# The MLPs of a decoder trunk: first matrix by weights-stationary columns, woven between the row blocks of the second

## The chip, the cores and the metric

The kernel runs on one core of one Trainium2 chip. The metric is device time in microseconds (us) of one execution; the median of several runs counts. The engines are called as in the profile: PE is TensorE (matmuls), PEld its weight loads, DVE VectorE, ACT ScalarE, POOL GpSimd, SP SyncE, which issues the DMAs of the weights.

## The reference

A decoder trunk of two layers on 256 tokens with a width of 2048, in float32. Layer 0 is a retention layer, layer 1 latent attention (MLA); each is followed by the same kind of MLP, which is what the change is about:

```python
def rms_norm(x, gain):
    y = xf * lax.rsqrt(jnp.mean(xf * xf, axis=-1, keepdims=True) + RMS_EPS)
    return y * gain

def sq_relu_mlp(h, w1, w2):
    return jnp.square(jax.nn.relu(h @ w1)) @ w2      # w1: 2048 x 8192, w2: 8192 x 2048

for layer in range(2):
    x = x + (retention or mla)(rms_norm(x, ...))
    x = x + sq_relu_mlp(rms_norm(x, norm_mlp[layer]), mlp_w1[layer], mlp_w2[layer])
```

## The kernel before

**Precision.** Every float32 operand is split in two fp32r parts, a high part (ACT casts it) and a low part (DVE subtracts): `split`, L180. A product is three matmuls: high by high, high by low, low by high.

**Two ways to multiply.** In the ordinary way the activations, 128 tokens by 128 features, are the stationary operand and the weights stream, 512 columns at a time, so the result has tokens on the partitions. `gemm_t` (L253) is the other way: 128 x 128 weights are stationary and the 256 tokens stream. There one 512-wide matmul takes the high weights over the high and the low activations, which lie side by side, and one 256-wide matmul the low weights over the high activations. The result has features on the partitions, the form in which the next product needs its activations, so no transpose is needed. Before the change only the query and key projections of the retention heads use it.

**Pairs and sevens.** `gemm_pair` (L329) makes two blocks of 512 columns for both blocks of 128 tokens. It goes over row blocks of 256 weight rows (`quad`, L280). A row block of the plain kind is eight products. One of the seven-product kind is seven products with sums of weight blocks (made by DVE, L312 to L317) and sums of activations (`with_sums`, L388). Its accumulators are c11, c12, c21 (three banks of the four "acc" banks of PSUM), c22 (the fourth), p1 and p5 (the two "tp" banks), and p6 and p7 (the two-bank tile "at"). `SEVEN = (3, 5, 7)` names the row blocks of the seven kind, three of eight. `pair_out` (L364) copies the accumulators out (ACT) and combines p1, p5, p6 and p7 (DVE).

**The MLP before (L770).** Four groups of 2048 hidden features each. Per group: two pairs of the first matrix (8 row blocks each, names u), after each of which the blocks are summed, scaled by the token's norm with a ReLU (ACT, L784), transposed on PE (`hid_tp`, L203: 16 per pair), squared, split, and for the row blocks in `SEVEN` summed. Then two pairs of the second matrix (8 row blocks each, names d). The eight parts of each of these pairs are added to x, which lies in DRAM (`x_home`), by accumulating DMAs that POOL issues (`to_home`, L143). In the last group x is brought into SBUF (`x_tiles`), the first pair is added to it there, and columns 1024 to 2047 are done as two plain products (`gemm`), so that only the last block's work is left at the end.

**Weights.** Each chunk is 1 MB (128 x 2048), brought by one DMA on SP's queue into one of three "raw" buffers; its high and low parts go into five "wh" and five "wl" buffers of 1024 columns each. A plain row block or a chunk of a plain product needs two of each, a seven-product row block four (one of them half used).

**Order.** The Python code emits instructions in an order with its own queue of due times (`later`, `tick`, `need`); the framework then orders each engine's instructions by its own estimate of when they can run. So the order on an engine isn't that of the source line by line, but each engine runs its list strictly in that order.

Of the kernel before, what the change touches and what calls it, by code (L numbers as in the profile page):

```python
# [11 lines left out]
F32 = mybir.dt.float32  # L12
# [4 lines left out]
ALU = mybir.AluOpType  # L17
# [18 lines left out]
P = 128  # L36
# [30 lines left out]
def yoco(ctx: ExitStack, tc: tile.TileContext, a):  # L67
# [63 lines left out]
    def x_tiles(name):  # L131


        def bring(b):
            both = act_tile(f"x_{name}{b}", F32)
            for t in range(NT):
                x[t][b] = both[:, t].rearrange("p i s -> p (i s)")
                nc.gpsimd.dma_start(x[t][b], x_home[t][b])

        for b in range(NB):  # L140
            later(2 * b, lambda b=b: bring(b))
# [8 lines left out]
    def into_x(done, c, p):  # L150
        for j in range(2):
            later(2 * j, lambda j=j: done(2 * p + j, [c[t][j] for t in range(NT)]))

    def gain(col):
        return gains[:, col : col + 1]
# [97 lines left out]
    def gemm_t(w, chunk0, act, nk, name, done):  # L253
# [3 lines left out]
        for g in range(n):  # L257
# [71 lines left out]
    def gemm_pair(w, chunk0, act, kinds, name, done):  # L329

        made = {}
        total, count = {}, {}
        for seven in kinds:
            for key in ("c11", "c12", "c21"):
                total[key] = total.get(key, 0) + (1 if seven else 2)
            for key in ("p1", "p5", "p6", "p7") if seven else ("c22", "c22"):
                total[key] = total.get(key, 0) + 1

        def get(key):
            if key not in made:  # L340
                if key in ("p6", "p7"):
                    both = two_banks(f"{name}_p67")
                    made["p6"], made["p7"] = both[:, 0], both[:, 1]
                else:
                    made[key] = bank("tp" if key[0] == "p" else "acc", [512], f"{name}_{key}")
            return made[key]

        def mm(key, lhs, rhs):
            dst, n = get(key), count.get(key, 0)
            count[key] = n + 1  # L350
            (ah, al), (bh, bl) = lhs, rhs
            nc.tensor.matmul(dst, ah, bh, start=n == 0, stop=False)  # L352
            nc.tensor.matmul(dst, ah, bl, start=False, stop=False)  # L353
            nc.tensor.matmul(dst, al, bh, start=False, stop=n == total[key] - 1)  # L354

        for i in range(len(kinds)):
            need(act, i + 1)
            v, more = act[i]
            quad(w, chunk0 + i, (v, more if kinds[i] else None), mm, f"{name}{i}")
            if i == len(kinds) - 1:  # L360
                queue.append((clock[0] + 1, -1, lambda: pair_out(made, name, done)))
            tick()

    def pair_out(c, name, done):  # L364

# [89 lines left out]
            r.append(rstd(tot, D, 1, f"{name}{t}"))  # L455
        return r

    def add_to_x(acc, b, ss, name):
        for t in range(NT):
            for part in acc[t] if isinstance(acc[t], tuple) else (acc[t],):  # L460
                nc.vector.tensor_tensor(x[t][b], part, x[t][b], op=ALU.add)
            if ss is not None:
                square_sum(x[t][b], ss[t][:, b : b + 1], f"{name}_{t}{b}")

    def into_next(ss, g0s, outs, r, name, sums=()):


        def done(b, acc):
            add_to_x(acc, b, ss, name)
# [220 lines left out]

    ss = [small(NB, f"ss1_{t}") for t in range(NT)]
    act, r = [], []
    into_n1 = into_next(ss, [G_MLP0], [act], r, "n1", SEVEN)
    halves = [[], []]

    def ret_projected(h, qk, gate, v, s):
# [71 lines left out]


    def mlp(layer, act, r, done):  # L770
        w1, w2 = a[f"mlp_w1_{layer}"], a[f"mlp_w2_{layer}"]
        f0 = 0
        for gi, nf in enumerate(GROUPS):
            hid, blocks = [], []
            kinds = [i in SEVEN for i in range(2 * nf)]
            last = gi == len(GROUPS) - 1

            def up(c, p, hid=hid, blocks=blocks):

                need(r, NT)  # L780
                c = summed(c)
                for t in range(NT):
                    for i in range(2):
                        nc.scalar.activation(c[t][i], c[t][i], AF.Relu, scale=r[t])  # L784

                def turn(i):
                    for q in (2 * i, 2 * i + 1):
                        name = f"hid{layer}_{p}{q}"
                        tp = transposed(
                            lambda t, j: c[t][q // 2][:, (q % 2 * 2 + j) * P : (q % 2 * 2 + j + 1) * P], f"{name}_tp"  # L790
                        )
                        u = f2k([2, S], f"{name}_u")
                        nc.scalar.activation(u, tp, AF.Square)
                        v = act_tile(name)
                        split_act(v, u)
                        blocks.append((v, with_sums(u, name) if len(blocks) in SEVEN else None))
                        hid.append(v)

                later(0, lambda: turn(0))
                later(1, lambda: turn(1))  # L800

            for p in range(f0 // 2, (f0 + nf) // 2):
                seven = SEVEN if p else SEVEN[1:]
                gemm_pair(
                    w1, p * 8, act, [i in seven for i in range(8)], f"u{layer}_{p}", lambda c, p=p, up=up: up(c, p)
                )
            if last:
                x_tiles(f"mlp{layer}")
            for p in range(2):
                if last and p:  # L810
                    for b in (2, 3):
                        need(hid, 2 * nf)
                        gemm(
                            a[f"mlp_w2t_{layer}"], (b - 2) * nf, hid, 4 * nf, 512, f"d{layer}_{gi}{b}",
                            lambda acc, b=b: done(b, acc),
                        )
                    continue

                def add(c, p=p, last=last):
                    into_x(done, c, p) if last else to_home(c, p)  # L820

                gemm_pair(w2, p * 32 + 2 * f0, blocks, kinds, f"d{layer}_{gi}{p}", add)
            f0 += nf

    ss = [small(NB, f"ss2_{t}") for t in range(NT)]
    act_kv, act_q, r2 = [], [], []
# [243 lines left out]
    for b in range(8):  # L1070
# [3 lines left out]
    act, r = [], []  # L1074
    x_tiles("wo")
    gemm_blocks(
        a["mla_w_o"], lambda b: b * 4, a["mla_w_op"], o_act, KD, "wo", into_next(ss, [G_MLP1], [act], r, "n3", SEVEN)
    )

    def finish(b, acc):  # L1080
        add_to_x(acc, b, None, "")
# [100 lines left out]
```

## Time and profile before

| | |
|---|---|
| runs | 2495.94, 2499.55 and 2505.04 us; median 2499.55 us |
| profiled execution | span 2497.0 us from the first to the last instruction; a time of its own beside the span is not given |
| PE | 2471.9 us busy (99%), 11683 matmuls |
| DVE, ACT, POOL | 2096.7 (84%), 1574.8 (63%), 252.2 us (10%) busy |
| DMA | 519.97 MB, mean 208 GB/s; 478.09 MB read from and 39.85 MB written to HBM |
| first MLP, second MLP | some 690 and 688 us of the span |

How to read it: names are those of the program without numbers, so `u_c` is any c accumulator of the first matrix and `d_wl` the low weights of the second. `x748` is a count; after the bar stand the busy time in us, the mean of one instruction in ns, and the idle time of the engine ahead of them with what ended it. Rows of windows give, for each engine, busy us and the number of instructions; then the granted clock of PE, the mean busy share of the 16 DMA engines, and GB/s. Rows of the timeline give start and duration in us. A matmul's end is modelled and overlaps the next one's start.

### The profile page before, as it was taken

How to read it: one execution, taken by the hardware profiler on the slowest of the kernel's cores; microseconds unless marked ns; L12 is line 12 of the kernel's file. 1: busy time of each engine (PE TensorE's matmuls, PEld its weight loads, DVE VectorE, ACT ScalarE, POOL GpSimd, SP SyncE). 2: the span in 40 equal slices, each digit the busy share in tenths (PEclk: the TensorE clock that was granted, in tenths of full speed). 3: DMA queues.
4: the chain of work that ended last, by engine and by line, in shares of the span. 5: the costliest groups of instructions: out<-in, count | busy, mean ns of one | idle time of the engine just before them, and what ended most of it. 6: DMA issues, size and time to landing. Idle time of an engine off the chain costs nothing.

```text
span 2497.0 us, 31492 instructions
## 1 busy us (share of the span) xinstructions
PE 2471.9 (99%) x11683; PEld 2075.1 (83%) x11683; DVE 2096.7 (84%) x2723; ACT 1574.8 (63%) x2228; POOL 252.2 (10%) x308
## 2 busy tenths in 40 slices
PE   8999999999999999999999999999999999999999
PEld 7788888888888888888888888998888888888887
DVE  7788888888898888889889888776899888898896
ACT  6566555555676657566666767666676566575663
POOL 6300011000010110110110101110010201101100
PEclk9999999999999999999999999999999999999999
DMA  8545568555565685775875555444455956857754
GB/s 290 211 173 202 178 217 246 183 193 196 211 217 189 207 263 186 235 237 186 247 259 191 197 196 189 159 149 163 173 213 203 262 203 213 249 187 233 258 200 165
DMA packets 92825, 519.97 MB, mean 208 GB/s; under 512 B 11009, under 2 KB 12161, under 8 KB 39425
## 3 DMA queue, kind: packets, MB, share of 16 engines
q1 hardware_dynamic: 71280, 471.78, 52.5%
q0 software_dynamic: 21248, 46.15, 8.9%
q8 instruction: 91, 1.49, 0.2%
q14 instruction: 62, 0.50, 0.1%
q10 hardware_dynamic: 144, 0.05, 0.0%
HBM read 478.09 MB, written 39.85 MB: 207 GB/s over the span
## 4 chain that ended last, share of the span: by engine, by line
PE 80%; DVE 10%; DMA 4%; ACT 4%; issue 2%; POOL 1%; ACTq 0%; SPq 0%; DVEq 0%; POOLq 0%
PE u_c L353 7%; PE u_c L354 7%; PE u_c L352 7%; PE d_c L353 4%; PE d_c L354 4%; PE d_c L352 4%; PE rp_c L353 3%; PE rp_c L354 3%; PE rp_c L352 3%; DVE d_wl L184 3%; PE ro_c L352 2%; PE ro_c L353 2%; PE ro_c L354 2%; PE rq_acc L272 2%; PE rk_acc L272 2%; DMA d_raw<-in_mlp_w 2%
## 5 line engine op out<-in xcount | busy, mean ns | idle before, releaser
L184 DVE TENSOR_TENSOR u_wl<-u_raw,u_wh 128x1024 fp32r<-128x1024 f32 (+1 forms) x256 | 280.0, 1124 | 35.8 <-ACT u_wh L183 35.8
L184 DVE TENSOR_TENSOR d_wl<-d_raw,d_wh 128x1024 fp32r<-128x1024 f32 (+1 forms) x256 | 283.4, 1132 | 26.0 <-ACT d_wh L183 25.1
L353 PE MATMUL u_c<-u_wl,n 128*128 128x512 f32 x748 | 291.8, 390 | 1.1 <-DVE u_wl L184 1.0
L352 PE MATMUL u_c<-u_wh,n 128*128 128x512 f32 x748 | 291.3, 391 | 0.0
L354 PE MATMUL u_c<-u_wh,n 128*128 128x512 f32 x748 | 291.3, 389 | 0.0
L183 ACT CAST u_wh<-u_raw 128x1024 fp32r<-128x1024 f32 (+1 forms) x256 | 238.9, 981 | 60.6 <-DMA u_raw<-in_mlp_w 27.2
L183 ACT CAST d_wh<-d_raw 128x1024 fp32r<-128x1024 f32 (+1 forms) x256 | 240.0, 991 | 56.3 <-DMA d_raw<-in_mlp_w 25.1
L353 PE MATMUL d_c<-d_wl,hid 128*128 128x512 f32 x644 | 251.4, 390 | 1.7 <-DVE d_wl L184 1.6
L352 PE MATMUL d_c<-d_wh,hid 128*128 128x512 f32 x644 | 252.1, 391 | 0.0
L354 PE MATMUL d_c<-d_wh,hid 128*128 128x512 f32 x644 | 250.9, 390 | 0.0
L183 ACT CAST u_wh<-u_u 128x1024 fp32r<-128x1024 f32 x92 | 94.2, 1050 | 153.5 <-DVE u_u L317 129.8
L183 ACT CAST d_wh<-d_u 128x1024 fp32r<-128x1024 f32 x84 | 84.9, 1049 | 162.6 <-DVE d_u L317 154.7
L353 PEld LDWEIGHTS u_c<-u_wl,n 128*128 128x128 f32 x748 | 140.5, 188 | 31.1 <-DVE u_wl L184 2.8
L354 PEld LDWEIGHTS u_c<-u_wh,n 128*128 128x128 f32 x748 | 140.4, 188 | 29.2
L352 PEld LDWEIGHTS u_c<-u_wh,n 128*128 128x128 f32 x748 | 140.4, 188 | 28.6
L183 ACT CAST rp_wh<-rp_raw 128x1024 fp32r<-128x1024 f32 x112 | 106.7, 972 | 67.7 <-PE rp_c L354 37.5
L184 DVE TENSOR_TENSOR u_wl<-u_u,u_wh 128x1024 fp32r<-128x1024 f32 x92 | 110.7, 1222 | 43.6 <-ACT u_wh L183 43.5
L353 PEld LDWEIGHTS d_c<-d_wl,hid 128*128 128x128 f32 x644 | 120.9, 188 | 29.0 <-DVE d_wl L184 4.5
L354 PEld LDWEIGHTS d_c<-d_wh,hid 128*128 128x128 f32 x644 | 120.9, 188 | 25.1
L352 PEld LDWEIGHTS d_c<-d_wh,hid 128*128 128x128 f32 x644 | 120.9, 188 | 24.6
L184 DVE TENSOR_TENSOR d_wl<-d_u,d_wh 128x1024 fp32r<-128x1024 f32 x84 | 99.9, 1222 | 35.9 <-ACT d_wh L183 35.9
L148 POOL DMA_DIRECT2D xh<-d_c x48 | 42.1, 1029 | 844.6 <-ACT d_c L369 844.5
(567 smaller groups left out, 6570.0 us busy)
## 6 DMA issues: line engine op xcount, KB each, us to landing
u_raw<-in_mlp_w SPq DMA_DIRECT2D x128, 1024.0 KB, 5.3
d_raw<-in_mlp_w SPq DMA_DIRECT2D x112, 1024.0 KB, 4.9
rp_raw<-in_ret_w_gv SPq DMA_DIRECT2D x56, 1024.0 KB, 4.9
ro_raw<-in_ret_w_out SPq DMA_DIRECT2D x32, 1024.0 KB, 4.9
uq_raw<-in_mla_w_uq SPq DMA_DIRECT2D x24, 768.0 KB, 4.1
rq_raw<-in_ret_w_qk SPq DMA_DIRECT2D x16, 1024.0 KB, 6.6
rk_raw<-in_ret_w_qk SPq DMA_DIRECT2D x16, 1024.0 KB, 4.8
d_raw<-in_mlp_w2t SPq DMA_DIRECT2D x16, 1024.0 KB, 5.1
```

The lines of the kernel that those rows point to most:

```text
L148: nc.gpsimd.dma_start(x_home[t][2 * p + j], part, accum_op=ALU.add)
L183: nc.scalar.copy(h, src)
L184: nc.vector.tensor_tensor(l, src, h.bitcast(F32), op=ALU.subtract)
L272: nc.tensor.matmul(acc[f], wh[:, cols], a.rearrange("p i s -> p (i s)"), start=k == 0, stop=k == nk - 1)
L352: nc.tensor.matmul(dst, ah, bh, start=n == 0, stop=False)
L353: nc.tensor.matmul(dst, ah, bl, start=False, stop=False)
L354: nc.tensor.matmul(dst, al, bh, start=False, stop=n == total[key] - 1)
```

## The change

- The MLP has eight groups of 1024 hidden features (`GROUPS, FB = 8, 8`: eight columns of 128 features).
- The first matrix is done the weights-stationary way. The first group: two halves of four columns each, 512 features from one chunk (`columns`); the second half's accumulators are the "at" and "tp" banks. All later groups: one column of 128 features at a time (`column`), a chunk of 128 columns by all 2048 rows, with one "acc" bank.
- The second matrix's pairs have four row blocks per group, of which 0, 1 and 2 (`WOVEN`) are of the seven kind; in the last group 0 and 2 (`ENDED`). After each row block (`pair_steps`) comes one column of the next group's first matrix.
- ReLU and square act on the unscaled sums; the squared scale of the token is applied where the result is added to x (`scalar_tensor_tensor` in `x_tiles` and `add_to_x`). The transposes of the hidden blocks and `summed` on the first matrix are gone.
- The pairs' parts are written or added by POOL's DMAs to a sum of its own in DRAM (`y_home`): p1, p5 and what is made of them one step before the other four. It is brought with x at the end.
- Sums of activations are no longer made for the norm ahead of an MLP (`into_next(..., SEVEN)`).
- The last group's first pair has four row blocks, the two plain products two chunks each.

```diff
-GROUPS = (4, 4, 4, 4)
+GROUPS, FB = 8, 8
+WOVEN, ENDED = (0, 1, 2), (0, 2)

 def bring(b):            # in x_tiles
...
         nc.gpsimd.dma_start(x[t][b], x_home[t][b])
+        if y_home is not None:
+            y = f2k([512], f"y_{name}{t}{b}")
+            nc.gpsimd.dma_start(y, y_home[t][b])
+            nc.vector.scalar_tensor_tensor(
+                x[t][b], y, scale[t], x[t][b], op0=ALU.mult, op1=ALU.add)

+    def column(w, chunk, act, nk, name, done):
+        acc = bank("acc", [512], f"{name}_acc")
+        need(act, nk // 2)
+        def use(half, wh, wl):
+            n = nk // 2
+            for j in range(n):
+                k = half * n + j
+                a = act[k // 2][:, k % 2]
+                turned(acc, wh, wl, slice(j * P, (j + 1) * P), a, k, nk)
+        stream(w, chunk, 2048, name, use, lambda: done(acc))
+
+    def turned(acc, wh, wl, cols, a, k, nk):
+        def low():
+            nc.tensor.matmul(acc[:, 0:S], wl[:, cols], a[:, 0], start=False, stop=False)
+        if k > 0:
+            low()
+        nc.tensor.matmul(acc, wh[:, cols], a.rearrange("p i s -> p (i s)"), start=k == 0, stop=k == nk - 1)
+        if k == 0:
+            low()
+
+    def columns(w, chunk0, act, nk, accs4, name, done):
+        n = nk // 4
+        for g in range(n):
+            need(act, 2 * g + 2)
+            def use(half, wh, wl):
+                for j in range(2):
+                    k = g * 4 + half * 2 + j
+                    a = act[k // 2][:, k % 2]
+                    for f in range(4):
+                        turned(accs4[f], wh, wl, slice(j * 512 + f * P, j * 512 + (f + 1) * P), a, k, nk)
+            stream(w, chunk0 + g, 2048, f"{name}{g}", use, (lambda: done(accs4)) if g == n - 1 else None)

+    def pair_steps(w, chunk0, act, kinds, name, put):
...
+        def get(key):
...
+                    made[key] = bank("acc" if key in ("c11", "c12", "c21") else "tp", [512], f"{name}_{key}")
...
+        def products_out():
+            o = {}
+            for key in ("p1", "p5"):
+                o[key] = f2k([512], f"{name}_{key}")
+                nc.scalar.copy(o[key], made[key])
+            v, u = (f2k([512], f"{name}_{i}") for i in "vu")
+            nc.vector.tensor_tensor(v, made["p6"], o["p1"], op=ALU.add)
+            nc.vector.tensor_tensor(u, made["p7"], v, op=ALU.add)
+            put(0, 0, o["p1"])
+            put(1, 0, u)
+            def rest():
+                nc.vector.tensor_tensor(v, o["p5"], v, op=ALU.subtract)
+                nc.vector.tensor_tensor(o["p5"], o["p5"], u, op=ALU.subtract)
+                put(0, 1, v)
+                put(1, 1, o["p5"])
+            later(0, rest)
+        def blocks_out():
+            for t, j in ((0, 0), (0, 1), (1, 0), (1, 1)):
+                key = f"c{t + 1}{j + 1}"
+                if key in made:
+                    o = f2k([512], f"{name}_{key}")
+                    nc.scalar.copy(o, made[key])
+                    put(t, j, o)
+        def step(i):
+            need(act, i + 1)
+            v, more = act[i]
+            quad(w, chunk0 + i, (v, more if kinds[i] else None), mm, f"{name}{i}")
+            if i == sevens - 1:
+                queue.append((clock[0] + 1, -2, products_out))
+            if i == len(kinds) - 1:
+                queue.append((clock[0] + 1, -1, blocks_out))
+            tick()
+        return [lambda i=i: step(i) for i in range(len(kinds))]

 def mlp(layer, act, r, done):
...
+        def up(acc, g, f):
+            i, j = divmod(f, 2)
+            if j == 0:
+                open_tiles[g, i] = f2k([2, S], f"hid{layer}_{g}{i}_u")
+            u = open_tiles[g, i]
+            nc.scalar.copy(u[:, j], acc[:, S:])
+            nc.vector.tensor_tensor(u[:, j], acc[:, 0:S], u[:, j], op=ALU.add)
+            if j == 0:
+                return
+            del open_tiles[g, i]
+            def square():
+                name = f"hid{layer}_{g}{i}"
+                nc.scalar.activation(u, u, AF.Relu)
+                nc.scalar.activation(u, u, AF.Square)
+                v = act_tile(name)
+                split_act(v, u)
+                seven = i in (WOVEN if g < GROUPS - 1 else ENDED)
+                blocks[g].append((v, with_sums(u, name) if seven else None))
+            later(0, square)
...
+        for half in range(2):
+            if half:
+                both = two_banks(f"u{layer}_b")
+                four = [both[:, 0], both[:, 1]] + [bank("tp", [512], f"u{layer}_b{i}") for i in range(2)]
+            else:
+                four = [bank("acc", [512], f"u{layer}_a{i}") for i in range(4)]
...
+            columns(first, 4 * half, act, KD, four, f"u{layer}_{half}", out)
+        scales()
+        for g in range(GROUPS - 1):
+            for p in range(2):
+                steps = pair_steps(
+                    w2, p * 32 + 4 * g, blocks[g], [i in WOVEN for i in range(4)], f"d{layer}_{g}{p}", put(p))
+                for i, step in enumerate(steps):
+                    step()
+                    f = 4 * p + i
+                    column(w1, g * FB + f, act, KD, f"u{layer}_{g + 1}{f}", lambda acc, g=g, f=f: up(acc, g + 1, f))
+        x_tiles(f"mlp{layer}", y_home, scale)
...
+        gemm_pair(
+            w2, 4 * (GROUPS - 1), blocks[-1], [i in ENDED for i in range(4)], f"d{layer}_{GROUPS - 1}0",
+            lambda c: into_x(last, c, 0, 1))
+        for b in (2, 3):
+            gemm(
+                a[f"mlp_w2t_{layer}"], (b - 2) * 2, hid, 8, 512, f"d{layer}_{GROUPS - 1}{b}",
+                lambda acc, b=b: last(b, acc))
```

`put` adds a part to `y_home`, or writes it where nothing stands yet; `last` keeps the blocks of the end in order.

More of the change, by code (lines that the diff above doesn't have):

```diff
@@ L770, in mlp @@
     def mlp(layer, act, r, done):
[L771 to L805, printed above, removed]
-                )
[L807 to L823, printed above, removed]
@@ new lines, in mlp, with scales @@
+        first, w1, w2 = a[f"mlp_w1a_{layer}"], a[f"mlp_w1_{layer}"], a[f"mlp_w2_{layer}"]
+        y_home = [[dram.tile([P, 512], F32, name=f"yh{layer}_{t}_{b}") for b in range(NB)] for t in range(NT)]
+        written = set()
+        blocks = [[] for _ in range(GROUPS)]
+        hid = Firsts(blocks[-1])
+        scale = []
+        def scales():
+            need(r, NT)
+            for t in range(NT):
+                q = small(1, f"rsq{layer}{t}")
+                nc.gpsimd.tensor_tensor(q, r[t], r[t], op=ALU.mult)
+                scale.append(q)
@@ new lines, in mlp, with last @@
+        ended = {}
+        def last(b, acc):
+            ended[b] = acc
+            for b in range(NB):
+                if b not in ended:
+                    return
+                if ended[b] is not None:
+                    done(b, ended[b], scale)
+                    ended[b] = None
+        gemm_pair(
+            w2, 4 * (GROUPS - 1), blocks[-1], [i in ENDED for i in range(4)], f"d{layer}_{GROUPS - 1}0",
+            lambda c: into_x(last, c, 0, 1),
+        )
+        for b in (2, 3):
+            gemm(
+                a[f"mlp_w2t_{layer}"], (b - 2) * 2, hid, 8, 512, f"d{layer}_{GROUPS - 1}{b}",
+                lambda acc, b=b: last(b, acc),
+            )
```

67 lines of the change are left out of this document (54 added, 13 removed).

## The prediction

> **What bounds the kernel now.** I read the page first (busy shares, slices, chain), then the stages of the two MLPs by windows, then the timeline of TensorE (PE).
>
> ```profile
> span 2497.0 us, 31492 instructions
> PE 2471.9 (99%) x11683; PEld 2075.1 (83%) x11683; DVE 2096.7 (84%) x2723; ACT 1574.8 (63%) x2228; POOL 252.2 (10%) x308
> PE 80%; DVE 10%; DMA 4%; ACT 4%; issue 2%; POOL 1%; ACTq 0%; SPq 0%; DVEq 0%; POOLq 0%
> ```
>
> PE is busy almost everywhere, and makes 80% of the chain; DVE is next with 84% busy. So an edit counts by the PE time that it takes out or puts in, plus the stalls that it makes or ends. The ends of matmuls are modelled, so I price matmuls by start to start.
>
> ```profile
> 733.51 0.39 PE L352 MATMUL u_c<-u_wh,n 128*128 128x512 f32 x1
> 1423.65 0.30 PE L244 MATMUL kd_acc<-kd_wh,n 128*128 128x320 f32 x1
> 1804.61 0.62 PE L352 MATMUL u_c<-u_wh,n 128*128 128x512 f32 x2
> 2492.45 0.39 PE L246 MATMUL d_acc<-d_wh,hid 128*128 128x512 f32 x1
> 907.72 0.39 PE L352 MATMUL u_c<-u_wh,n 128*128 128x512 f32 x1
> ...
> 909.76 0.39 PE L352 MATMUL u_c<-u_wh,n 128*128 128x512 f32 x1
> ```
>
> The MLPs run from 733.51 to 1423.65 and from 1804.61 to 2492.68 (last start plus one step): 690.1 + 688.1 = 1378.2 us. From 907.72 to 909.76 lie nine matmuls of 512 columns: 0.2267 us each. Everything outside the MLPs keeps its PE work; the sums dropped from the two norms ahead of them were DVE and ACT work beside a full PE, and I cost them at nothing.
>
> **The change, part by part: PE.** By the code, one row block of a pair by eight products is 24 matmuls, by seven 21. The first matrix was 8 pairs of 8 blocks with 23 sevens per MLP: 23 x 21 + 41 x 24 = 1467. The second was 7 pairs with 3 sevens in 8 plus 192 plain ones: 1473. Together 5880 in both MLPs.
>
> - First matrix, new: 64 columns x 16 row blocks = 1024 couples per MLP of one 512-wide and one 256-wide matmul. The projections of the retention heads already run this couple:
>
> ```profile
> 301.46 0.40 PE L272 MATMUL rk_acc<-a,rk_wh 128*128 128x512 f32 x1
> ...
> 309.93 0.40 PE L272 MATMUL rk_acc<-a,rk_wh 128*128 128x512 f32 x1
> 44.97 0.40 PE L272 MATMUL rk_acc<-a,rk_wh 128*128 128x512 f32 x1
> ...
> 54.33 0.39 PE L272 MATMUL rk_acc<-a,rk_wh 128*128 128x512 f32 x1
> ```
>
> 24 couples in 8.47 us are 0.3529 each; in the first head 27 in 9.36 us are 0.3467. The later heads all keep the slower step, so I take 0.3529: 2048 x 0.3529 = 722.7, against 2934 x 0.2267 = 665.1 removed: **+57.6**. With 0.3467 it would be +44.9.
>
> The Trainium skill has a rule against this: "Larger matmuls are more efficient than smaller matmuls, when possible" (Perfetto Trace Analysis, Matmuls). The trace agrees: as long matmuls the same columns would take 1.5 x 0.2267 = 0.340 per couple, so splitting them costs 0.013, or 26 us of the 57.6; at one price per column the first matrix would cost 31.
>
> - Second matrix: per group of 1024 features two pairs of 3 x 21 + 24 = 87; last group 2 x 21 + 2 x 24 = 90 plus 96 plain. 7 x 174 + 186 = 1404, so 69 fewer per MLP: 138 x 0.2267 = **-31.3**.
>
> - Transposes of the hidden blocks: 256 go, as 32 runs of 8.
>
> ```profile
> 953.29 1.03 PE L203 MATMUL hid_tp<-cst,u_c 128*128 128x128 f32 x8
> 954.08 0.48 PE L352 MATMUL u_c<-u_wh,n 128*128 128x512 f32 x1
> 954.39 0.40 PE L353 MATMUL u_c<-u_wl,n 128*128 128x512 f32 x1
> 996.57 1.25 PE L203 MATMUL hid_tp<-cst,u_c 128*128 128x128 f32 x8
> 997.57 0.47 PE L352 MATMUL d_c<-d_wh,hid 128*128 128x512 f32 x1
> 997.89 0.39 PE L353 MATMUL d_c<-d_wl,hid 128*128 128x512 f32 x1
> ```
>
> A run costs 0.79 and the matmul after it 0.31 in place of 0.23, so 0.87; in the other form 1.00 + 0.09 = 1.09. 32 runs are 28 to 35; most are of the first form: **-30**.
>
> PE work as such: 57.6 - 31.3 - 30 = **-3.7 us**. What is gained by fewer transposes and products is spent on shorter matmuls.
>
> **Stalls.** Of the 1378.2 us, 5880 x 0.2267 = 1333.0 are products, 30 hidden transposes, and 56 transposes of x at about 0.11 are 6: **9 us** of stalls and seams remain. Where they come from:
>
> ```profile
> PE d_c L353 <- DVE d_wl L184: 1.6, 4, 0.5
> PE d_acc L245 <- DVE d_wl L184: 1.4, 2, 0.9
> PE u_c L353 <- DVE u_wl L184: 1.0, 2, 0.8
> core 0: us, PE busy (x) PEld busy (x) DVE busy (x) ACT busy (x) POOL busy (x), PEclk, DMA share, GB/s
> 1920.00:1930.00 10.00, 10.00 (x46) 8.28 (x45) 8.77 (x10) 5.37 (x6) 0.00 (x0) 1.00 0.58 204
> 1930.00:1940.00 10.00, 10.00 (x46) 8.29 (x45) 7.81 (x9) 9.27 (x13) 3.58 (x4) 1.00 0.90 205
> 1940.00:1950.00 10.00, 10.00 (x46) 8.29 (x45) 7.53 (x9) 2.90 (x4) 3.49 (x4) 1.00 1.04 333
> 1950.00:1960.00 10.00, 9.45 (x43) 7.48 (x42) 8.74 (x10) 5.37 (x6) 0.00 (x0) 1.00 0.79 218
> 1930.69 4.97 DMA d_raw<-in_mlp_w
> 1938.35 7.61 DMA d_raw<-in_mlp_w
> 872.92 9.77 DMA d_raw<-in_mlp_w
> 1946.05 1.57 ACT L183 CAST d_wh<-d_raw 128x1024 fp32r<-128x1024 f32 x2 [4.72 <-DMA d_raw<-in_mlp_w]
> ```
>
> The windows, in which the granted clock is 1.00 throughout, show one end of a pair of the second matrix. Its eight parts go out as accumulating DMAs from POOL; the DMA share goes from 0.58 to 1.04, a weight chunk that took 4.97 us takes 7.61 (9.77 at worst), ACT waits 4.72 for it, DVE follows, and in the fourth window PE loses 0.55. PE waits eight times in the MLPs, 4.0 us in all (a little more by starts), never over 0.9. The excess share over 0.58 in the burst, 0.32 + 0.46 + 0.21 of 10 us, is 9.9 us of all engines, 1.24 per part.
>
> After: 14 pairs per MLP write parts, not 6, so 28 such bursts in place of 12. Four parts of each leave a step and a column earlier than the other four, as blunt a burst as now. Average share per group: 0.58 + 16 x 1.24 / 84.7 = 0.81, now 0.69:
>
> ```profile
> 906.00:1076.00 170.00, 169.97 (x765) 140.48 (x764) 148.71 (x168) 108.36 (x140) 13.87 (x17) 1.00 0.69 223
> 991.00:1076.00 85.00, 84.97 (x382) 69.92 (x381) 74.90 (x87) 54.34 (x71) 9.14 (x11) 1.00 0.72 227
> ```
>
> So there is room on average (84.7 is 174 x 0.2267 + 128 x 0.3529), and bursts bite. Loss per burst: 0 to 0.9 by the rows; about 4 us in 12 bursts and two last stages give 0.3, which I take: 28 x 0.3 = 8.4.
>
> The Trainium skill states that DMAs started from different engines end on the same 16 DMA engines and interleave (DMA: Bandwidth & Descriptors, Issuing engines are not separate DMA queues). The windows agree: parts from POOL lengthen SP's weight loads.
>
> DVE, per half group (four steps, four columns, 42.4 us of PE):
>
> ```profile
> L184 DVE TENSOR_TENSOR d_wl<-d_raw,d_wh 128x1024 fp32r<-128x1024 f32 x25 | 29.6, 1219 | 1.9 <-ACT d_wh L183 1.8
> L316 DVE TENSOR_TENSOR d_u<-d_u,d_raw 128x512 f32<-128x512 f32 x6 | 4.1, 686 | 0.1
> L183 ACT CAST d_wh<-d_raw 128x1024 fp32r<-128x1024 f32 x24 | 24.2, 1062 | 5.2 <-DMA d_raw<-in_mlp_w 3.9 <-ACT d_wh L183 0.7 <-PE d_c L354 0.6
> L369 ACT COPY d_c<-d_c 128x512 f32<-128x512 f32 x8 | 4.4, 589 | 0.3 <-PE d_c L354 0.3
> ```
>
> 1.18 us per 1024-wide operation (29.6 / 25), 0.68 per 512-wide. A seven-product step is four and three: 6.8; a plain step or a column two: 2.4. 3 x 6.8 + 2.4 + 4 x 2.4 = 32.4; column sums, splits of the hidden blocks and sums of products are some twelve 512-equivalents, 8. These means overlap by some 7% (the groups of the stage 991 to 1076 sum to 80 where 74.9 were busy), so 37.6 of 42.4: 89%, where that stage has 88%. ACT by its rows: 19 wide casts, 6.5 half casts, ten copies and squares, some 30 of 42.4, up from 64% to about 70%. Neither becomes the bound.
>
> New wait: the ACT copy of a column's sums waits for PE to end the column, and the next column's casts stand behind it. These need a wh buffer that the same column frees (five buffers: four of the step, and that half), so they lose nothing, and PE has a step of 4.8 us before it needs them, against at most 0.6 + 1.0 (the rows of ACT) and 1.2 of DVE. DVE's first sum of a later step is placed ahead of that column's low parts; if its load is late, the low parts wait behind it. That is the path by which a burst reaches PE. POOL's issues (9.1 us for 11 instructions in the stage's row, 16 parts per group after) are hidden by its idle time.
>
> Seams: at an MLP's start the columns want x blocks 2 and 3 sooner (blocks 6 and 7 of 8 after 3 x 16 couples, 17 us, not after 6 row blocks, 31), and the two last gemms are half as long: 1 us at each of four seams, 0 to 3.
>
> Sum: -3.7 - 9 + 8.4 + 4 = **-0.3 us** on the span of 2497.0. The median of the runs is 2499.55, 2.55 above the span, so **2499 us**.
>
> **The rivals.**
> 1. *Slower: late loads.* Seven-product steps follow each other three times, and the loss per burst is the 0.9 of the worst rows: 28 x 0.9 = 25 in place of 8.4, so 2516. It decides from 0.55 per burst (+7.5). For it: DMA already saturates in bursts, and each new group has twice as many. Against: most bursts cost PE nothing now.
> 2. *Faster: the short step.* The couple runs at 0.3467 (-12.7), as in the first head, bursts cost 0.2 (-2.8): 2484. For it: columns are short runs between others, as the first head's are not locked to the slower step. Against: all later heads.
> 3. *It doesn't do what it says:* interleaving smooths nothing, since the stage with the most DVE work stalls PE under 1 us in 85; time stays. This is part of my forecast.
>
> **How the numbers follow.** About 0.3% (7.5 us) is what a measurement of this kernel can tell from no change. Forecast with the third rival, 2492 to 2507: 0.43. Rival 1, above: 0.30. Rival 2, below: 0.27. Lowest: 0.3467, no burst loss, seams 0: 2499 - 12.7 - 8.4 - 4 = 2474; highest: 0.9 per burst, seams 3 each: 2499 + 17 + 8 = 2524. The range leaves out a tenth at each end: 2481 to 2518. The likeliest case's own range is 2492 to 2507.
>
> **What would show it.** Right: couples of 512 and 256 columns at 0.35 in the columns; no hidden transposes; 84 to 86 us per group; DVE near 89%; DMA share near 0.8, with full tenths twice per group. Wrong: couples off 0.347 to 0.353; PE waiting on the low parts after each burst by over 0.55; PE waiting on ACT's copy of a column; or a DVE share over 95%.

## The result, and the profile after

| | before | changed |
|---|---|---|
| median | 2498.14 us (4 runs beside the changed kernel) | 2517.0 us (2515.47 to 2521.58, 4 runs) |
| ratio | | 1.0071, 95% interval 1.0054 to 1.0089 |
| profiled span | 2497.0 us | 2514.7 us |

The change costs 0.7%, some 18 us. The forecast was no change (2499 us). First the page of the changed kernel: span and busy shares.

```profile
span 2514.7 us, 33723 instructions
PE 2474.7 (98%) x12451; PEld 2104.3 (84%) x12451; DVE 2126.7 (85%) x2873; ACT 1620.6 (64%) x2366; POOL 366.1 (15%) x456
```

On the page hardly anything has moved: PE 98% in place of 99%, DVE 85% in place of 84%. A loss of 18 us in 2500 is not to be found in shares; it has to be placed. So next the stages, by the starts of matmuls on PE's timeline (start, duration). `u_a` opens an MLP, the `d_` rows are the first matmuls of groups, 1375.39 and 2458.44 open the last ones, and the rows at 1427.82 and 2509.97 end the MLPs.

```profile
732.00 0.39 PE L308 MATMUL u_a<-n,u_wh 128*128 128x512 f32 x1
...
780.24 0.40 PE L433 MATMUL d_c<-d_wh,hid_more 128*128 128x512 f32 x1
...
949.64 0.39 PE L433 MATMUL d_p<-d_wh,hid 128*128 128x512 f32 x1
...
1034.27 0.39 PE L433 MATMUL d_p<-d_wh,hid 128*128 128x512 f32 x1
...
1375.39 0.39 PE L399 MATMUL d_p<-d_wh,hid 128*128 128x512 f32 x1
...
1427.82 0.31 PE L251 MATMUL kd_acc<-kd_wh,n 128*128 128x320 f32 x1
...
1815.97 0.63 PE L308 MATMUL u_a<-n,u_wh 128*128 128x512 f32 x2
...
1864.12 0.40 PE L433 MATMUL d_c<-d_wh,hid_more 128*128 128x512 f32 x1
...
2458.44 0.39 PE L399 MATMUL d_p<-d_wh,hid 128*128 128x512 f32 x1
...
2509.97 0.39 PE L253 MATMUL d_acc<-d_wh,hid 128*128 128x512 f32 x1
```

- A woven group takes 1034.27 - 949.64 = 84.63 us, against 84.7 priced. All seven of an MLP take 595.2 and 594.3, 85.0 a group.
- The last group takes 52.4 us in the first MLP and 51.8 in the second. Its own work is 186 matmuls of 0.2267, 42.2 us.
- The MLPs are 695.8 and 694.2 us, together 11.8 more than the 1378.2 of before. Between them lie 388.2 us, where 1423.65 to 1804.61 were 381.0: 7.2 more. The first MLP starts 1.5 sooner.

So the woven stage does what was forecast, and the loss is in the two last groups and in what follows the first of them. PE's largest wait in the MLPs (total, times, longest) and, as one window, four woven groups (busy us of PE, PEld, DVE, ACT and POOL, then the granted clock, the DMA share and GB/s):

```profile
PE d_c L400 <- DVE d_wl L191: 12.0, 2, 6.1
```

```profile
865.00:1204.00 339.00, 339.00 (x1724) 288.02 (x1723) 304.19 (x376) 230.92 (x318) 52.88 (x61) 1.00 0.83 248
```

Two stalls of 6 us, one in each last group, are all that the MLPs have of size; no other wait in them is over 1.2. Before, none was over 0.9. In the woven stage PE is busy 339.00 of 339.00, DVE 304.19 (89.7%), ACT 68%, and the DMA share is 0.83. Now DVE's timeline at the first stall: start, duration, and in brackets the idle time ahead with what ended it.

```profile
1382.99 0.69 DVE L191 TENSOR_TENSOR d_wl<-d_raw,d_wh 128x512 fp32r<-128x512 f32 x1
1392.17 0.75 DVE L143 SCALAR_TENSOR_TENSOR x_mlp<-y_mlp,rsq,x_mlp 128x512 f32<-128x512 f32 x1 [8.50 <-DMA x_mlp<-xh]
1392.84 1.22 DVE L191 TENSOR_TENSOR d_wl<-d_u,d_wh 128x1024 fp32r<-128x1024 f32 x1
1393.98 2.07 DVE L143 SCALAR_TENSOR_TENSOR x_mlp<-y_mlp,rsq,x_mlp 128x512 f32<-128x512 f32 x3
```

The multiply-add that brings y into x (L143) stands in DVE's list between low parts of the last pair's weights. It waits 8.50 us for its load, and the low parts behind it, which need nothing but what is already there (ACT has cast both sums by 1384.13), wait with it. The tile's own view gives the loads of x, when POOL issued the first and the last, and the time from issue to landing (shortest, median, longest):

```profile
L139 POOL DMA_DIRECT2D x_mlp<-xh x8: 536/536/541, 1380.0 to 1390.1; - x8
DMA to landing us min/median/max: 6.7/10.0/12.0
```

The loads are not only slow, they are also issued late: in POOL's list they stand behind the last parts. POOL issues the last of these at 1376.24, and the first load of x at 1380.0.

And PE, then the windows with the granted clock (the column ahead of the DMA share):

```profile
1387.63 0.39 PE L399 MATMUL d_c<-d_wh,hid 128*128 128x512 f32 x1
1394.12 0.80 PE L400 MATMUL d_c<-d_wl,hid 128*128 128x512 f32 x1 [6.10 <-DVE d_wl L191]
...
1395.14 0.63 PE L399 MATMUL d_p<-d_wh,hid_more 128*128 128x512 f32 x1
...
1396.42 0.63 PE L399 MATMUL d_p<-d_wh,hid_more 128*128 128x512 f32 x1
...
1397.79 0.39 PE L401 MATMUL d_p<-d_wh,hid_more 128*128 128x512 f32 x1
```

```profile
1388.00:1392.00 4.00, 0.02 (x1) 0.00 (x0) 0.00 (x0) 1.25 (x2) 1.07 (x2) 0.86 1.01 408
1392.00:1394.00 2.00, 0.00 (x0) 0.00 (x0) 1.83 (x3) 0.00 (x0) 1.07 (x2) 0.50 1.02 383
1394.00:1396.00 2.00, 1.89 (x5) 1.50 (x6) 2.00 (x5) 0.00 (x0) 0.00 (x0) 0.50 0.99 375
1396.00:1398.00 2.00, 1.81 (x5) 1.01 (x4) 2.00 (x3) 1.04 (x1) 0.00 (x0) 0.57 0.23 86
```

PE's wait is paid twice. It stands for 6.1 us, and the granted clock falls to 0.50 meanwhile: from 1395.14 to 1396.42 three matmuls take 0.427 us each. From 1387.63, the last start ahead of the stall, to 1397.79 PE starts eight matmuls; that takes 10.16 us, and 1.81 at full clock. So the stall costs 8.3 us, 6.1 of standing and the rest of half clock, which with the group's own 42.2 and 16 transposes for the next norm makes up its 52.4. In the second MLP a stall of 5.88 us costs more: the last group's 51.8 are 9.6 over its matmuls.

The Trainium skill gives 426.7 ns as the step of 512 columns while the clock is halved, and an idle window of about 3.4 us as what halves it (TensorE: Matmul & The Clock Gate, Part 1); the step in this trace, 427 ns, agrees. The clock falls 2.9 us after PE stops in the first MLP and 5.3 us after in the second (last section).

### The profile page after: what moved, and what is told of

The parts are those of the page before. It is cut to its first block, busy times and chain, and to the rows that moved or that the text cites. A ratio compares the mean times of both kernels' runs of the same rounds, so it can differ in the third digit from the quotient of the medians.

```text
span 2514.7 us, 33723 instructions
## 1 busy us (share of the span) xinstructions
PE 2474.7 (98%) x12451; PEld 2104.3 (84%) x12451; DVE 2126.7 (85%) x2873; ACT 1620.6 (64%) x2366; POOL 366.1 (15%) x456
## 4 chain that ended last, share of the span: by engine, by line
PE 82%; DVE 7%; DMA 5%; ACT 3%; issue 2%; POOL 1%; DVEq 0%; SPq 0%; ACTq 0%; POOLq 0%
PE u_acc L308 15%; PE u_acc L304 8%; PE d_c L435 4%; PE d_c L434 4%; PE d_c L433 4%; PE rp_c L400 3%; PE rp_c L401 3%; PE rp_c L399 3%; PE d_p L433 3%; PE d_p L434 3%; PE d_p L435 3%; DMA d_raw<-in_mlp_w 2%; PE ro_c L399 2%; PE ro_c L401 2%; PE ro_c L400 2%
## 5 line engine op out<-in xcount | busy, mean ns | idle before, releaser
L308 PE MATMUL u_acc<-n,u_wh 128*128 128x512 f32 x1792 | 642.5, 398 | 0.4 <-ACT d_wh L190 0.4
L304 PE MATMUL u_acc<-n,u_wl 128*128 128x256 f32 x1792 | 485.8, 281 | 2.3 <-DVE u_wl L191 2.2
L308 PEld LDWEIGHTS u_acc<-n,u_wh 128*128 128x128 f32 x1792 | 336.7, 188 | 78.4 <-ACT d_wh L190 0.7
L304 PEld LDWEIGHTS u_acc<-n,u_wl 128*128 128x128 f32 x1792 | 337.9, 189 | 13.3 <-DVE u_wl L191 5.2
L191 DVE TENSOR_TENSOR u_wl<-u_raw,u_wh 128x1024 fp32r<-128x1024 f32 x256 | 306.9, 1218 | 29.1 <-ACT u_wh L190 28.6
L190 ACT CAST u_wh<-u_raw 128x1024 fp32r<-128x1024 f32 x256 | 267.9, 1051 | 15.4 <-PE u_a L308 9.1
L435 PE MATMUL d_c<-d_wh,hid 128*128 128x512 f32 x392 | 152.5, 389 | 0.0
L433 PE MATMUL d_c<-d_wh,hid 128*128 128x512 f32 x392 | 152.5, 389 | 0.0
L399 PE MATMUL rp_c<-rp_wh,a 128*128 128x512 f32 x322 | 126.5, 393 | 0.5 <-DVE rk_u L737 0.5
L191 DVE TENSOR_TENSOR rp_wl<-rp_raw,rp_wh 128x1024 fp32r<-128x1024 f32 x112 | 121.3, 1117 | 5.9 <-ACT rp_wh L190 5.4
L400 PE MATMUL rp_c<-rp_wl,a 128*128 128x512 f32 x322 | 125.5, 390 | 0.4 <-DVE rp_wl L191 0.4
L401 PE MATMUL rp_c<-rp_wh,a 128*128 128x512 f32 x322 | 125.5, 390 | 0.0
```

The source lines that it names most:

```text
L190: nc.scalar.copy(h, src)
L191: nc.vector.tensor_tensor(l, src, h.bitcast(F32), op=ALU.subtract)
L304: nc.tensor.matmul(acc[:, 0:S], wl[:, cols], a[:, 0], start=False, stop=False)
L308: nc.tensor.matmul(acc, wh[:, cols], a.rearrange("p i s -> p (i s)"), start=k == 0, stop=k == nk - 1)
```

## The experiments

Theory A: DVE's list stands while a load is on its way, with low parts behind it; the half clock follows. Theory B: the accumulating bursts cost PE throughout. Theory C: somebody has to wait for those loads, and a wait removed in one place comes back in another. Medians stand beside the kernel before in the same comparison.

| kernel | us | before | ratio, 95% interval |
|---|---|---|---|
| e1_late | 2511.62 | 2500.56 | 1.0048 (1.0033 to 1.0063) |
| e7_free | 2494.47 | 2500.56 | 0.9976 (0.9966 to 0.9987) |
| e2_direct | 2489.99 | 2500.56 | 0.9960 (0.9946 to 0.9974) |
| e3_apart | 2510.20 | 2500.56 | 1.0039 (1.0026 to 1.0052) |
| e4_noparts | 2487.98 | 2498.52 | 0.9956 (0.9939 to 0.9973) |
| e5_two | 2510.67 | 2498.52 | 1.0046 (1.0031 to 1.0061) |
| e6_unwoven | 2650.56 | 2498.52 | 1.0608 (1.0592 to 1.0623) |
| e8_four | 2642.47 | 2498.52 | 1.0574 (1.0558 to 1.0590) |
| e9_pool | 2520.81 | 2496.84 | 1.0097 (1.0081 to 1.0114) |

### e1_late: the same work, later in DVE's list

```diff
 # x_tiles, for each b and t
+if b < 2:
+    ys[t, b] = y
+    continue
 nc.vector.scalar_tensor_tensor(x[t][b], y, scale[t], x[t][b], ...)
 # add_to_x
-for part in parts:
+for part in (*parts, ys.pop((t, b))) if (t, b) in ys else parts:
```

> The changed kernel with one edit: for the first two column blocks of x, DVE's multiply-add of y into x is given after the blocks of the last pair have been added, so that in DVE's list it stands behind every low part of the last group's second matrix; loads, bursts and matmuls stay. Theory A (the loss is DVE's multiply-add at the head of its list, waiting 12 us for x and y while the low parts of weights queue behind it, with the half clock that follows): the stalls of 6.1 and 5.9 us on d_c at 1394 and 2477 are gone, and with them the half clock behind them, 8 to 10 us per MLP, so 2497 to 2502 us. Theory B (the loss is the 56 bursts of accumulating DMAs, contention with the weight loads, which this kernel keeps): 2513 to 2518. Theory C (the loss comes back as another wait in the last group, the adds of the blocks now done later): 2505 to 2514, with a new stall on DVE behind the last pair.

Theory C came true: 2511.6, some 5 us under the changed kernel, about as much as the two intervals can tell apart. The stalls on d_c are gone. In the second MLP DVE's timeline and PE's show what took their place:

```profile
2477.84 2.08 DVE L582 SCALAR_TENSOR_TENSOR x_mlp<-d_c,rsq,x_mlp 128x512 f32<-128x512 f32 x3 [2.81 <-ACT d_wh L195]
...
2492.17 4.62 DVE L196 TENSOR_TENSOR d_wl<-d_raw,d_wh 128x1024 fp32r<-128x1024 f32 x4
```

```profile
2493.44 0.80 PE L257 MATMUL d_acc<-d_wl,hid 128*128 128x512 f32 x1 [7.34 <-DVE d_wl L196]
```

From 2477.84 to 2492.17 DVE adds blocks without a pause, over 14 us, and only then makes the low parts of the last weights, so PE stands for 7.34. The wait for the load is gone, but the adds are still ahead of the low parts: it is what stands ahead of them in the list that costs, a wait or work.

### e7_free: the same list, the last bursts left out

```diff
 def add(t, j, part):
+    if g == GROUPS - 2:
+        return
```

> The changed kernel without the accumulating DMAs of the seventh group of each MLP (so these products are missing from the sum): 32 of 224 parts in each MLP, the two bursts that stand ahead of the loads of x and y. DVE's list is the same as in the changed kernel. Theory A (the multiply-add waits because its loads stand behind the last bursts): the loads land in some 3 us instead of 12, the stalls of 6 us on d_c are gone or under 1 us, 2497 to 2503 us. If the loads are slow by themselves: the stall stays at 3 us or more, and 2508 to 2517. Theory B (the bursts cost PE about evenly): an eighth to a seventh of the loss, 2514 to 2516.

2494.5, and no stall in the last groups. (What is left out are 16 of the 112 parts of each MLP, 32 of 224 in both.) DVE's list is that of the changed kernel, but the multiply-add no longer waits (no bracket). The loads of x, in the view of their line:

```profile
1383.89 0.74 DVE L143 SCALAR_TENSOR_TENSOR x_mlp<-y_mlp,rsq,x_mlp 128x512 f32<-128x512 f32 x1
```

```profile
L139 POOL DMA_DIRECT2D x_mlp<-xh x8: 538/538/538, 1362.0 to 1365.7; - x8
DMA to landing us min/median/max: 3.1/9.0/13.8
```

Theory A has the stall right, the time within 3 us, and the loads wrong. They don't land in 3 us; their median is 9.0, hardly less than the 10.0 of the changed kernel. But without the last parts ahead of them in POOL's list they are issued 18 us sooner, from 1362.0 and not from 1380.0, and have landed before DVE comes to the multiply-add at 1383.89. So the loads are late because they are issued late. The last groups now take 44.1 us (1375.53 to 1419.59) and 42.4 (2448.01 to 2490.40), though the eight multiply-adds are still there: their work alone costs nothing here, their wait did.

Two bursts less in each MLP give 22 us back. Either they cost some 5.6 us each, which nothing else bears out, or the wait behind them was the price. e2_direct and e4_noparts decide that.

### e2_direct: all bursts, late loads, and no multiply-add of y

```diff
-nc.scalar.copy(o[key], made[key])
+for t in range(NT):
+    nc.scalar.activation(o[key, t], made[key], AF.Copy, scale=scale[t])
...
-nc.gpsimd.dma_start(y_home[t][b], part, accum_op=ALU.add)
+nc.gpsimd.dma_start(x_home[t][2 * p + j], part, accum_op=ALU.add)
...
-x_tiles(f"mlp{layer}", y_home, scale)
+x_tiles(f"mlp{layer}")
```

> The changed kernel with the sum back in x: each part is multiplied by the token's squared scale as it is copied out (two more copies on ACT and one more add on DVE per pair) and accumulated straight into x, so there is no y, no load of y and no multiply-add of y on DVE. Bursts, columns, couples and matmuls stay. Theory A: no wait on DVE's list in the last group, the MLPs at 684 to 688 us each where they now take 694 to 696: 2496 to 2502 us, and below 2498 if the stalls between the MLPs go with it. Theory B (bursts): 2512 to 2518. Theory C (work of ACT and DVE is what holds the woven stage): slower than the changed kernel, 2520 or more.

2490.0: 27 us under the changed kernel and 0.4% under the one before (interval 0.26% to 0.54%), so this version beats both. That is 6 us under theory A's forecast. The loads of x in the view of their line, the windows of the first MLP's last group, and PE's waits in the whole of that MLP:

```profile
L139 POOL DMA_DIRECT2D x_mlp<-xh x8: 538/712/897, 1375.9 to 1382.8; - x8
DMA to landing us min/median/max: 8.2/10.8/12.9
```

```profile
1380.00:1388.00 8.00, 8.00 (x37) 6.60 (x36) 6.83 (x9) 5.18 (x6) 1.60 (x3) 1.00 1.03 410
1388.00:1396.00 8.00, 8.00 (x37) 6.63 (x36) 6.79 (x9) 6.14 (x10) 0.00 (x0) 1.00 1.01 390
```

```profile
PE u_b L308 <- ACT u_wh L190: 0.3, 1, 0.3
```

This is the clearest evidence of the study. The loads are as slow as in the changed kernel (median 10.8 us, there 10.0) and issued only 4 us sooner, the DMA share is as high (1.03 and 1.01), and PE is busy 8.00 of 8.00. Here slow loads and full DMAs cost nothing, with no instruction that waits for them ahead of work that PE needs. ACT and DVE do more than in the changed kernel (1662.7 and 2142.2 us on the page), without loss. PE's rows:

```profile
780.57 0.40 PE L433 MATMUL d_c<-d_wh,hid_more 128*128 128x512 f32 x1
...
1373.04 0.39 PE L399 MATMUL d_p<-d_wh,hid 128*128 128x512 f32 x1
...
1417.14 0.39 PE L253 MATMUL d_acc<-d_wh,hid 128*128 128x512 f32 x1
...
1850.16 0.40 PE L433 MATMUL d_c<-d_wh,hid_more 128*128 128x512 f32 x1
...
2442.73 0.39 PE L399 MATMUL d_p<-d_wh,hid 128*128 128x512 f32 x1
...
2484.67 0.39 PE L253 MATMUL d_acc<-d_wh,hid 128*128 128x512 f32 x1
```

The last groups take 44.3 and 42.2 us, 8.1 and 9.6 less. The seven woven groups take 592.5 and 592.6, 2.7 and 1.8 less. Between the MLPs it is 4.2 less. These make the gain.

### e3_apart: summed apart, alone, in the kernel before

```diff
 # x_tiles of the kernel before
+y = f2k([512], f"y_{name}{t}{b}")
+nc.gpsimd.dma_start(y, y_home[t][b])
+nc.vector.tensor_tensor(x[t][b], y, x[t][b], op=ALU.add)
 # the parts
-nc.gpsimd.dma_start(x_home[t][2 * p + j], part, accum_op=ALU.add)
+nc.gpsimd.dma_start(home[t][2 * p + j], part, accum_op=ALU.add)
```

> The kernel before with one part of the change alone: the second matrix's parts are accumulated in a y of their own, and x and y are loaded and added on DVE in the last group. Groups, tiles, matmuls and bursts stay those of before, where the last burst lies some 80 us ahead of the loads. Theory A (the wait arises because the changed kernel's last burst stands right ahead of the loads): little, within 4 us of the kernel before, no stall over 2 us on the last group's matmuls. Theory D (summing apart costs by itself, through the second load and DVE's list): 8 to 20 us slower than before.

I had it wrong: 9.7 us slower (6.5 to 13), as theory D said. The first pair of the first MLP's last group as one window, here and in the kernel before:

```profile
1335.49:1383.37 47.88, 45.70 (x201) 35.08 (x199) 45.66 (x62) 30.30 (x43) 5.84 (x11) 1.00 0.67 236
```

```profile
1332.87:1376.41 43.54, 43.53 (x200) 35.96 (x199) 40.53 (x52) 29.79 (x43) 0.00 (x0) 1.00 0.54 194
```

The pair takes 4.3 us more for the same matmuls, and in the second MLP 4.4 more (47.96 for 43.54). That is 8.8 of the 13.4 us by which this profiled span is longer. DVE has ten instructions and 5.1 us of work more in it, eight of them the adds of y, and is busy for 45.66 of 47.88 us. It waits for no load there, and PE's waits are short, none over 0.7 us. So in the kernel before, where DVE is nearly full at this place (40.53 of 43.54), the adds cost by their work, not by a wait; summing apart costs some 10 us also without woven columns. The rest of the loss lies outside these pairs and isn't settled.

### e4_noparts: the price of the bursts

```diff
+if g:
+    return
 nc.gpsimd.dma_start(x_home[t][2 * p + j], part, accum_op=ALU.add)
```

> The direct version (e2_direct, 2490 us) with the accumulating DMAs of the parts given only in the first group of each MLP: 24 of the 28 bursts are left out (so the sums of the other six groups are missing from x), all else stays. Theory A (a burst beside woven columns costs next to nothing, since the woven groups show hardly a stall): 0 to 3 us less than e2_direct, 2487 to 2490. The prediction's term (0.3 us a burst): 7 us less, 2481 to 2485. The prediction's first rival (0.9 us a burst): 22 us less, 2468.

24 of 28 bursts less give 2 us by the medians and 1 us by the ratios: under 0.1 us each, though the two intervals alone would allow nearly 0.3. The traces are sharper. The first matmuls of the first woven group and of the last group, in the first MLP:

```profile
779.99 0.40 PE L433 MATMUL d_c<-d_wh,hid_more 128*128 128x512 f32 x1
...
1372.47 0.39 PE L399 MATMUL d_p<-d_wh,hid 128*128 128x512 f32 x1
```

The seven woven groups take 592.48 us without the bursts of six of them, and 592.47 with all of them in e2_direct. Theory B falls, and with it the first rival's price of 0.9; the 0.3 of the forecast was too much as well.

### e5_two and e8_four: what bounds the woven stage

```diff
-WOVEN, ENDED = (0, 1, 2), (0, 2)
+WOVEN, ENDED = (0, 1), (0, 2)        # e5_two
+WOVEN, ENDED = (0, 1, 2, 3), (0, 2)  # e8_four
```

> The direct version with 2 of 4 steps by 7 products in the woven groups where it has 3: 28 pairs of 3 more matmuls of 0.2267 us each on PE, and some 11 us less of DVE in a group of 86. If the woven groups are PE's alone (theory A): 19 us more than e2_direct, 2507 to 2511. If DVE or the DMAs hold part of a group, the lighter DVE gives some of it back: 2490 to 2502.

> The direct version with all 4 steps by 7 products in the woven groups where it has 3: PE has 2 times 3 matmuls of 0.2267 us less in each of 14 groups, 19 us in all; DVE gets two more weight blocks of sums and low parts and one more of the hidden's, some 11 us a group on top of 79 of 86 (91.6% busy in e2_direct's woven stage). If DVE is the next bound, as this sum says: its 90 us a group stand against PE's 85, so 30 to 70 us slower than e2_direct, 2520 to 2560, with waits of PE on d_wl and d_wh in every group. If PE alone sets the group: 2467 to 2475.

With two steps by seven products it is 21 us more than e2_direct, where the count of matmuls says 19: PE's alone. With four it is some 153 us more. PE's largest wait in e8_four, and four of its woven groups as a window:

```profile
PE d_c L433 <- ACT d_wh L190: 49.2, 52, 1.0
```

```profile
865.00:1204.00 339.00, 316.88 (x1510) 256.56 (x1509) 308.87 (x391) 223.73 (x309) 43.38 (x51) 0.96 0.73 214
```

Now PE waits 52 times for high parts, twice in nearly every pair: ACT casts sums that DVE has to make first. The direction was right, the size two to five times too small. The sum counted DVE's excess in busy time, but DVE is busy for 308.87 of 339 us (91%) here, no fuller than in e2_direct. What PE waits for is a chain, DVE's sum, ACT's cast, DVE's low part, that comes too late at each step; and the sum left out the lower clock beside these waits (0.96 in the window, 1.00 in e2_direct's). How much each makes isn't split. Of two, three and four steps, three is best.

### e6_unwoven: the order alone

```diff
 for i, step in enumerate(steps):
     step()
-    column(w1, g * FB + 4 * p + i, ...)
+for f in range(FB):              # after both pairs
+    column(w1, g * FB + f, ...)
```

> The direct version with the order alone changed: the eight columns of the next group come after both pairs, not one after each step of a pair. PE's, DVE's and ACT's work is the same. If weaving carries the arrangement (three steps of 7 products run DVE some 2 us a step behind PE, and there is no column between them to catch up on): stalls on d_c and d_p in every group, 2 to 6 us in each of 14 groups, 2520 to 2580. If it doesn't: within 4 us of e2_direct, 2486 to 2494.

Some 161 us more than e2_direct with the same work, and 70 beyond the forecast's upper end. PE's largest wait, a stretch of its timeline and the window around that:

```profile
PE d_c L433 <- ACT d_wh L190: 73.6, 56, 1.8
```

```profile
1001.65 0.50 PE L433 MATMUL d_c<-d_wh,hid 128*128 128x512 f32 x1 [1.73 <-ACT d_wh L190]
...
1004.27 0.63 PE L433 MATMUL d_p<-d_wh,hid_more 128*128 128x512 f32 x1
...
1005.12 0.63 PE L434 MATMUL d_p<-d_wl,hid_more 128*128 128x512 f32 x1
```

```profile
1000.00:1010.00 10.00, 7.60 (x23) 5.22 (x23) 7.61 (x9) 5.16 (x6) 2.46 (x3) 0.83 1.07 224
```

This wait is 74 of the 161, some 5 us in each of 14 groups, as forecast. Two steps in 0.85 us and a granted clock of 0.83 in these 10 us show that stretches at half clock are part of the rest; it isn't split further here. So the weaving is what lets three of four steps go by seven products, and it does smooth DVE's load, against the third rival.

### e9_pool: y added by GpSimd

```diff
-nc.vector.scalar_tensor_tensor(x[t][b], y, scale[t], x[t][b], op0=ALU.mult, op1=ALU.add)
+nc.gpsimd.tensor_scalar(y, y, scale[t], None, op0=ALU.mult)
+nc.gpsimd.tensor_tensor(x[t][b], y, x[t][b], op=ALU.add)
```

> The changed kernel with y kept, its bursts and its loads, but y scaled and added into x by GpSimd (two instructions of some 2.1 and 1.3 us a block, by the rows of GpSimd's 128x512 operations) where DVE had one: DVE's list has no instruction left that waits for the loads before the blocks of the last pair. Theory A (what costs is that DVE's list stands while the loads are on their way, and the place that eight multiply-adds take in it): the stalls of 6 us on d_c are gone and none of over 3 us comes in DVE's place, 2494 to 2502 us. Theory C (the loads themselves, late by their place behind the bursts, must be waited for by someone): the adds of the last blocks wait for GpSimd instead, 2505 to 2515, with a stall of PE on DVE or a later end.

Theory A's number fell and theory C's came, even 6 us beyond its range: 2520.8. DVE's row and PE's in the second MLP:

```profile
2490.69 2.08 DVE L575 SCALAR_TENSOR_TENSOR x_mlp<-d_c,rsq,x_mlp 128x512 f32<-128x512 f32 x3 [9.64 <-POOL x_mlp L144]
```

```profile
2500.02 0.79 PE L251 MATMUL d_acc<-d_wl,hid 128*128 128x512 f32 x1 [8.90 <-DVE d_wl L190]
```

DVE has no instruction of its own for y any more, and waits for POOL's: its first add of a block needs POOL's x, stands ahead of the low parts of the last weights, and holds them 9.64 us, and the adds behind it 8 us more. The waiter has changed, the list it stands in has not. In the first MLP DVE waits 9.49 us in the same way, and PE has its waits at the norm behind (4.8 and 3.9 us for the transposes). The mechanism of A and the warning of C are one: what counts is what stands ahead of DVE's low parts, and above all whether it waits.

## Why the prediction was wrong, point by point

| step of the prediction | forecast | measured |
|---|---|---|
| woven group: 174 matmuls and 128 couples | 84.7 us | 84.63 |
| DVE, ACT, DMA share in it | 89%, 70%, 0.81 | 89.7%, 68%, 0.83 |
| loss per burst | 0.3 us | none to be seen (592.48 and 592.47 us, e4_noparts and e2_direct) |
| wait of the column's copies for PE | nothing | no wait of PE names them |
| seams, and the end of an MLP | 1 us each, 0 to 3 | last groups 8.1 and 9.6 us over e2_direct |
| outside the MLPs | nothing | +5.9 (17.7 on the span, 11.8 in the MLPs) |

**The step that failed** is the sentence "Seams: ... 1 us at each of four seams, 0 to 3". It counted the sooner need of x blocks and the shorter gemms, and left out what the change puts into the last group: DVE's multiply-adds of y into x, each with two loads ahead of it. The term was 4 us in all; the two stalls and their half clock cost some 8.3 and 9.6. The part on waits looked at the copies of the columns and at DVE's sums, both harmless, and never asked what is queued behind this one. Its price was on hand. A weight load beside a burst took up to 9.77 us in the trace of before, two bursts stand right ahead of the loads in POOL's list, and a wait on DVE holds the low parts, which PE reaches within a step of 4.8 us. From these rows I would now estimate a stall of some 5 us. The half clock was there too: in the kernel before, between the MLPs, PE stands 3.28 us until 1714.95, and its clock is 0.50 from 1713.5 to 1720.3.

**What was right.** The couple's price, the second matrix's saving and the hidden transposes together give the group to 0.1 us (its terms, summed exactly, make 84.6). With the multiply-add out of the way, the MLPs take 685.0 and 683.6 us in e2_direct (by the rows, with the first `u_a` at 732.34 and 1801.34): 9.6 less than before, where matmuls and old stalls were forecast to give 12.7 ahead of bursts and seams.

**The rivals.** The first came nearest in time (2516), for a wrong reason: its bursts and late loads of weights cost nothing. That 2517.0 lies inside the stated 2481 to 2518 is luck: the upper part of that range comes from this rival's price per burst. The loads that were late are those of x and y, twice, not 28 times. The second's short step did not come: the group's 84.63 less 174 x 0.2267 leaves 0.353 for each of 128 couples. The third is refuted by e6_unwoven.

**What stays open.** Between the MLPs the changed kernel is 7.2 us longer than before. 4.2 of it are gone in e2_direct and 3.7 in e7_free, the two kernels without a stall in the last group, so they probably hang on that. 3.0 stay in e2_direct. PE's waits there sum to 7.8 us, against 6.5 before, and a second run of eight of the norm's 32 transposes stands behind the MLP's end where only one did (16 and 8 of them), some 0.9 us by the price of the prediction. Neither was tried alone.

## What to carry to other kernels

When a change adds an instruction that waits for a DMA, look up where it stands in its engine's list, and price what stands behind it: the wait less the lead that the bound engine has, plus the half clock if that engine stands for some microseconds. Look up in the list of the issuing engine, too, what the load itself stands behind. A full DMA and a load of 12 us cost nothing by themselves; in e2_direct both are there, and PE's waits in that MLP sum to 0.3 us. It is worth paying for with steady work on an engine with room, here some more copies on ACT, to have no such instruction at the end of a stage, and moving it to another engine or further down helped little or not at all (e9_pool, e1_late), since what depends on it, or the work itself, still stood ahead of the low parts.

## What the runs showed of the hardware that was not expected

- The half clock does not begin and end with the stall. In windows of half a microsecond the granted clock is 0.50 from 1390.9 to 1397.7 at the first stall and from 2476.3 to 2483.2 at the second, 6.8 us each time. But it began 2.9 us after PE stopped in the one and 5.3 us after in the other. So more of it fell on running matmuls in the second, and the shorter stall was the dearer one: 5.9 us cost 9.6, 6.1 cost 8.3. Elsewhere it lasted 3.4 us (e6_unwoven, 1003.5 to 1006.9) and 10.2 (e1_late, 2488.5 to 2498.7), so all four are near a multiple of 3.4.
- Shorter waits come with it as well: in e6_unwoven a wait of 1.73 us is followed, 2 us after PE has resumed, by matmuls 0.43 us apart, and its run has a mean clock of 0.987, where e2_direct has 0.998. The Trainium skill's advice is to leave no gap over some 3 us between matmuls (TensorE: Matmul & The Clock Gate, Why this matters for your kernels); here shorter ones, one after the other, are dear too.
- A load of 256 KB took 3 to 14 us from issue to landing whether a burst stood right ahead of it or not: 6.7 to 12.0 in the changed kernel, 3.1 to 13.8 in e7_free without the last bursts. What the bursts set was when POOL issued it.
